# Attention on one core: VectorE's exponentials worked in 16-bit words, the order of the work kept

## The chip, the core and the metric

The kernel runs on one core of a Trainium2 chip. A core has five engines that each run their own queue in order: TensorE (PE in the profile, with its weight loads as PEld), VectorE (DVE), ScalarE (ACT), GpSimd (POOL) and SyncE (SP, which issues DMAs). The metric is the device time of one execution in microseconds.

## The reference

For 8 batches of 8 heads, with 512 positions of 64 numbers each, all in float32:

```python
scale = 1.0 / np.sqrt(q.shape[-1])
scores = np.einsum('bhqd,bhkd->bhqk', q, k) * scale
scores = scores - scores.max(axis=-1, keepdims=True)
attn = np.exp(scores)
attn = attn / attn.sum(axis=-1, keepdims=True)
return np.einsum('bhqk,bhkd->bhqd', attn, v).astype(np.float32)
```

## The kernel before

The 64 heads are taken as 32 pairs g = 0 to 31. A pair's q, k and v come in by one DMA each (256 KB), and GpSimd casts them to float16 (`cast`, steps `cq`, `ck`, `cv`). Pairs up to 21 have q and k transposed by TensorE into PSUM (`T`) and copied out by VectorE (`C`, tiles `tp` and `tqk`); from pair 22 a DMA transposes them (`u`).

A score group m is two blocks of 128 keys by 512 queries, 1024 elements per partition. TensorE writes it into one of three PSUM buffers `st` (`S`, as in `S12.0`: group 12, buffer 0). There are four groups to a pair. Nearly all groups get their exponential from ScalarE in one instruction (L295), which writes a float16 tile `pt`. No maximum is subtracted; the sum comes from a column of ones beside v.

Fourteen groups get their exponential on VectorE instead, by bit work in fixed point: the integer part of the scaled score is to become the exponent, and a polynomial in the fraction corrects the mantissa. The table `KIND` lists them with four kinds. For kinds C, F and S two matmuls first add a constant to the scores (the lift, L275), so that the bits of the 32-bit word in PSUM can be read as two halves. Each such group runs as steps between other work:

- `r` (`raise_`, L317): a pass over `st` that writes `z`, 32 bits;
- `p.0`, `p.1`, `p.2` (`pass_`, L350 and L331): passes that read halves of `st` or `z`, the intermediate `y`, and at last write the result, `pd` (32-bit words, of which TensorE reads every other half) or `pt`;
- for kinds S and X `m` (`middle`, L365 and L368) in the place of `p.1`: two instructions on GpSimd.

So ten groups (C and F) take four VectorE passes, and four groups (S and X) take three and two of GpSimd.

The values step `V` multiplies a block of 128 queries with v: four matmuls into one of seven places of an accumulator `o`, one of two PSUM banks that the transposes use as well. When seven are done, VectorE takes the reciprocal of the sums (`R`, tile `rc`) and multiplies (`N`, into `ring`); a DMA stores whole heads (`O`).

What runs after what on each engine is written out by hand as one list of steps, `ORDER`; every engine's queue follows it. A step such as `ck7+p12.2` is a cast that may not start before that VectorE step has ended.

```python
    def cast_behind(name, g, behind):
        ins = cast(g, name)
        if behind:
            tc.add_manual_dep(ins.ins, named[behind].ins.name, SYNC, reason="SBUF ports")
```

Of the kernel before, what the change touches and what calls it, by code (L numbers as in the profile page):

```python
# [8 lines left out]
FP32 = mybir.dt.float32  # L9
FP16 = mybir.dt.float16  # L10
U16 = mybir.dt.uint16
U32 = mybir.dt.uint32

LIFTED = "CFS"

EXP = mybir.ActivationFunctionType.Exp
AluOp = mybir.AluOpType
# [3 lines left out]
KIND = {5: "C", 12: "C", 20: "C", 30: "C", 39: "C", 47: "C", 57: "F", 68: "S", 72: "C", 81: "C", 93: "X", 99: "S", 108: "X", 111: "C"}  # L21
# [34 lines left out]
ck23 V11.0.3.95.0 T19.1.1 V11.1.0.96.0 cq24 V11.1.1.97.0 S71.1 R91.7 S72.0 m68.0 N91.7 S73.2 u22 C19  # L56
# [16 lines left out]
cv25+C2 V20.0.0.164.1 S98.2 N154.7 S99.1 m93.0 u29 S100.0 r99 V20.0.1.165.1 V20.0.2.166.1  # L73
# [3 lines left out]
V22.0.0.180.1 V22.0.1.181.1 S104.1 O133.1 R175.7 m99.0 S105.0 N175.7 V22.0.2.182.0 O147.1  # L77
# [7 lines left out]
N203.7 lv31 V24.1.3.215.0 m108.0 S117.0 p111.0 O189.1 V26.1.0.216.0 V26.1.1.217.1 O203.1  # L85
# [15 lines left out]
def kernel(  # L101
# [7 lines left out]
    nc = tc.nc  # L109
    B, H, S, D = q.shape  # L110
    P = 128
    NI = S // P
    assert NI == 4 and D == 64 and S == 512
    scale = float(D) ** -0.5
    LOG2E = 1.4426950408889634
# [14 lines left out]
    raises = {}  # L130
    for m, kind in KIND.items():
        (g, c, _), (g2, c2, _) = groups[m]
        assert 0 < g == g2 < LAST and c == c2
        if kind in LIFTED:
            raises.setdefault(g, set()).add(c)
# [6 lines left out]
    dpool = ctx.enter_context(tc.tile_pool(name="pd", bufs=4))  # L142
# [10 lines left out]
    lift = cpool.tile([P, P], FP16, name="lift")  # L153
# [10 lines left out]
    raised = {}  # L164
# [26 lines left out]
    def cast(g, name):  # L191
        if g >= NP:
            return
        if name == "v":
            return nc.gpsimd.tensor_copy(  # L195
                out=vps[g % NV][:, :, :, 0:D], in_=raw[g]["v"][:, :, :, :]
            )
        if g not in qkp:
            qkp[g] = qpool.tile([P, 2, NI, P], FP16, tag="qkp", name=f"qkp_{g}")
        dst = qkp[g][:, "qk".index(name)].rearrange("p i (h d) -> p h i d", h=2)  # L200
        src = raw[g][name]
        if (g, name) == (1, "q"):
            dve(nc.vector.tensor_copy(out=dst[:, :, 0:2], in_=src[:, :, 0:2]))
            return nc.gpsimd.tensor_copy(out=dst[:, :, 2:4], in_=src[:, :, 2:4])
        if name == "k" and g in raises:
            return nc.gpsimd.tensor_scalar(  # L206
                out=dst, in0=src[:, :, :, :], scalar1=128.0 * LOG2E, scalar2=1.0, op0=AluOp.mult, op1=AluOp.mult
            )
        return nc.gpsimd.tensor_copy(out=dst, in_=src[:, :, :, :])  # L209
# [7 lines left out]
    def dve(ins):  # L217
        latest[:] = [ins]
        return ins
# [42 lines left out]
    def scores(m, b):  # L262
        grp, kind = groups[m], KIND.get(m)
        half = m - len(groups) + 2
        cols = slice(256 * half, 256 * half + 256) if half >= 0 else slice(0, S)
        st = buffer(b, f"st_{m}")
        if kind in ("X", "Q"):
            bits = ppool.tile([P, 2, S], U16, tag="pt", name=f"pt_{m}")
            pt = bits.bitcast(FP16)
        elif kind:  # L270
            bits = dpool.tile([P, 2, S], U32, tag="pd", name=f"pd_{m}")
            pt = bits.bitcast(FP16).rearrange("p x (s n) -> p x s n", n=2)[:, :, :, 0]
            for x, (_, _, h) in enumerate(grp):
                s = slice(64 * h, 64 * h + 64)
                nc.tensor.matmul(st[:, x, :], lift[s], ones[s, 0:S], start=True, stop=False)  # L275
        elif half == 1:
            pt = last["pt"]
        else:
            pt = last["pt"] = ppool.tile([P, 2, S], FP16, tag="pt", name=f"pt_{m}")
        for x, (g, c, h) in enumerate(grp):  # L280
            if g == 0:
                s = slice(64 * (c % 2), 64 * (c % 2) + 64)
                kc = first["kt"][s, h, c // 2, :]
                qc = first["qt"][s, h].rearrange("p i c -> p (i c)")
            else:
                s = slice(64 * h, 64 * h + 64)
                kc = tqk[g][s, 1, c * P : (c + 1) * P]
                qc = tqk[g][s, 0, :]
            nc.tensor.matmul(st[:, x, cols], kc, qc[:, cols], start=kind is None or kind not in LIFTED, stop=True)  # L289
            blocks[(g, c, h)] = pt[:, x, :]  # L290
        if kind:
            raised[m] = {"st": st, "bits": bits}
            return
        by = scale / (128.0 * LOG2E) if grp[0][0] in raises else scale
        nc.scalar.activation(  # L295
            out=pt[:, :, cols], in_=st[:, :, cols], func=EXP, scale=by
        )
# [7 lines left out]
    LIFT = (143.0 * 1024 / 32, 0.0, -4.0 / 64)  # L305
    CUBIC = (-1.00024088 * 2.0**16, 3.90705425 * 2.0**16, 7.78636933e-2 * 1024 * 2.0**-48)
    QUARTIC = (7.77974906 * 2.0**16, -8.78105033 * 2.0**32, 4.4655924e-3 * 1024 * 2.0**-64)

    def fraction(t):
        return t.bitcast(U16).rearrange("p x (s n) -> p x s n", n=2)[:, :, :, 0]  # L310

    def raise_(m):
        r, kind = raised[m], KIND[m]
        r["z"] = wpool.tile([P, 2, S], FP32, tag="z", name=f"z_{m}")
        lifted = kind in LIFTED
        dve(
            nc.vector.tensor_scalar(  # L317
                out=r["z"][:, :, :],
                in0=r["st"][:, :, :],
                scalar1=2.0**17 if lifted else 1.0 if groups[m][0][0] in raises else 128.0 * LOG2E,  # L320
                scalar2=None if lifted else 143.0 * 1024,
                op0=AluOp.max if lifted else AluOp.mult,
                **({} if lifted else {"op1": AluOp.add}),
            )
        )

    def pass_(m, s):
        r, kind = raised[m], KIND[m]
        if kind in ("X", "Q") and s == 2:
            dve(  # L330
                nc.vector.scalar_tensor_tensor(  # L331
                    out=r["bits"][:, :, :],
                    in0=r["z"][:, :, :],
                    scalar=-(2.0**17) - QUARTIC[2] * (QUARTIC[1] / 2) ** 2,
                    in1=r["y"][:, :, :],
                    op0=AluOp.add,
                    op1=AluOp.add,
                )
            )
            return  # L340
        f, low = fraction(r["z"]), fraction(r["st"])
        if s == 0:
            r["y"] = wpool.tile([P, 2, S], FP32, tag="y", name=f"y_{m}")
        y = r["y"][:, :, :]
        last = s == 2
        quartic = kind in ("S", "X")
        zero = low if kind in LIFTED else f
        one = low if kind == "C" else f
        dve(
            nc.vector.scalar_tensor_tensor(  # L350
                out=r["bits"][:, :, :] if last else y,
                in0=(zero, one, y)[s],
                scalar=(QUARTIC if quartic else CUBIC)[s],
                in1=(f, y, r["z"][:, :, :])[s],
                op0=AluOp.mult if last else AluOp.add,
                op1=AluOp.add if last else AluOp.mult,
            )
        )

    def middle(m, _):  # L360
        r, kind = raised[m], KIND[m]
        t = wpool.tile([P, 2, S], FP32, tag="t", name=f"t_{m}", bufs=1)

        def product(x, add, scale, by=None):
            nc.gpsimd.tensor_scalar(  # L365
                out=t[:, :, :], in0=x, scalar1=add, scalar2=scale, op0=AluOp.add, op1=AluOp.mult
            )
            nc.gpsimd.tensor_tensor(  # L368
                out=r["y"][:, :, :], in0=t[:, :, :], in1=t[:, :, :] if by is None else by, op=AluOp.mult
            )  # L370

        if kind == "S":
            product(r["y"][:, :, :], QUARTIC[1], 1.0, r["y"][:, :, :])
            return
        centre = QUARTIC[1] / 2
        if kind == "Q":
            r["y"] = wpool.tile([P, 2, S], FP32, tag="y", name=f"y_{m}")
            product(fraction(r["z"]), QUARTIC[0] / 2, 1.0)
            centre -= (QUARTIC[0] / 2) ** 2
        product(r["y"][:, :, :], centre, QUARTIC[2] ** 0.5)  # L380
# [185 lines left out]
    with tc.manual_schedule():  # L566
# [4 lines left out]
        nc.vector.memset(lift, LIFT[0])  # L571
        for p in (32, 96):
            nc.vector.memset(lift[p : p + 32], LIFT[1])
            nc.vector.memset(lift[p : p + 1], LIFT[2])
        for n in range(NV):
# [10 lines left out]
            "m": middle,  # L586
# [48 lines left out]
```

## Time and profile before

| what | value |
|---|---|
| median of 3 runs | 116.33 us (116.09 to 116.99) |
| profiled execution | 116.05 us, span 114.3 us |
| granted TensorE clock | 1.000 |
| ScalarE busy | 107.0 us (94%) |
| VectorE busy | 103.5 us (91%) |
| TensorE matmuls busy | 103.8 us (91%) |
| GpSimd busy | 76.5 us (67%) |
| GpSimd casts of v, mean | 768 ns, 32 of them |
| GpSimd casts of q, mean | 612 ns, 30 of them |

The span runs from the first instruction to the last; the execution's own time has some 1.75 us around it. A line of the profile names the source line, the engine, the operation and `out<-in`. In a timeline the first number is the start, the second the duration, both in us, and in brackets stands the idle time before, with what ended it. Merged instructions show as xcount. Successive instructions of one engine overlap a little, so the distance from start to start is a better price than the duration.

### The profile page before, as it was taken

The page shows a single profiled execution, that of the slowest core. Times are in us where ns is not written, and L with a number is a line of the kernel's source. Part 1 is how long each engine was busy: PE and PEld are TensorE (multiplying, and loading weights), DVE is VectorE, ACT ScalarE, POOL GpSimd, SP SyncE. Part 2 cuts the span into 40 slices and gives each one's busy share as a digit, 9 for nine tenths or more (in the row PEclk, how much of TensorE's full clock was granted, in tenths as well). Part 3 has the DMA queues.
Part 4 walks back from the last instruction along what each step waited for, and adds up shares of the span by engine and source line. Part 5 has one row for each costly group of instructions (what it writes and reads, how often), then busy time and mean ns, then how long its engine had stood idle before and what let it go on. Part 6 is the DMA issues. An engine that isn't in the chain of part 4 may idle for free.

```text
span 114.3 us, 3938 instructions
## 1 busy us (share of the span) xinstructions
PE 103.8 (91%) x1549; PEld 65.7 (57%) x1549; DVE 103.5 (91%) x178; ACT 107.0 (94%) x119; POOL 76.5 (67%) x110
## 2 busy tenths in 40 slices
PE   7979899998899898999998899999999999999970
PEld 5635555565564564655665466675567666676660
DVE  4457999999999999999999999999999999999660
ACT  4499999999999999999999999999999999999960
POOL 2348755295968957927749999991799999384300
PEclk9999999999999999999999999999999999999999
DMA  2999999999999999999999998989959899999864
GB/s 92 276 317 373 384 380 382 383 385 373 384 388 367 363 382 382 372 384 388 373 376 383 373 215 260 172 267 384 272 147 312 238 327 151 383 333 366 290 231 146
DMA packets 45619, 36.44 MB, mean 319 GB/s; under 512 B 12704, under 2 KB 45600, under 8 KB 45600
## 3 DMA queue, kind: packets, MB, share of 16 engines
q1 hardware_dynamic: 45168, 35.86, 103.8%
q10 hardware_dynamic: 432, 0.33, 0.9%
q8 instruction: 12, 0.20, 0.6%
q14 instruction: 7, 0.06, 0.1%
HBM read 25.17 MB, written 8.39 MB: 294 GB/s over the span
## 4 chain that ended last, share of the span: by engine, by line
DVE 32%; PE 31%; ACT 26%; issue 5%; DMA 2%; ACTq 0%
ACT pt L295 24%; PE o L420 14%; PE st L289 13%; DVE y L350 12%; DVE tqk L254 5%; DVE ring L393 4%; DVE pd L350 4%; DVE z L317 4%; DMA q<-in_q_dram 2%; ACT pt L527 2%; DVE rc L385 1%; PE tp L234 1%; PE o L430 1%; DVE obl L461 1%; PE st L275 0%
## 5 line engine op out<-in xcount | busy, mean ns | idle before, releaser
L295 ACT ACTIVATE pt<-st 128x1024 f16<-128x1024 f32 (+1 forms) x112 | 102.1, 1113 | 0.4 <-PE st L289 0.4
L289 PE MATMUL st<-tqk 64*128 64x512 f16 (+1 forms) x250 | 47.0, 380 | 5.2 <-ACT pt L295 3.3
L420 PE MATMUL o<-vp,pt 128*128 128x65 f16 x912 | 45.4, 195 | 0.0
L420 PEld LDWEIGHTS <-pt 128*128 128x128 f16 x912 | 36.2, 98 | 14.4 <-issue 13.3
L195 POOL CAST vp<-v 128x512 f16<-128x512 f32 x32 | 24.1, 768 | 10.4 <-DVE pd L350 4.2
L289 PEld LDWEIGHTS <-tqk 64*128 64x128 f16 x250 | 14.4, 93 | 17.9 <-issue 8.2
L393 DVE TENSOR_TENSOR ring<-o,rc 128x448 f32<-128x448 f32 (+2 forms) x37 | 22.5, 608 | 1.0 <-DVE rc L385 0.2
L209 POOL CAST qkp<-q 128x512 f16<-128x512 f32 x30 | 18.1, 612 | 2.9 <-DVE rc L385 1.4
L317 DVE TENSOR_SCALAR z<-st 128x1024 f32<-128x1024 f32 x14 | 17.0, 1213 | 1.3 <-PE st L289 1.1
L209 POOL CAST qkp<-k 128x512 f16<-128x512 f32 x19 | 13.6, 719 | 5.7 <-issue 2.4
L350 DVE SCALAR_TENSOR_TENSOR pd<-y,z 128x1024 uint32<-128x1024 f32 x12 | 15.3, 1272 | 0.0
L420 PE MATMUL o<-vp,pd 128*128 128x65 f16 x96 | 15.1, 195 | 0.1
L350 DVE SCALAR_TENSOR_TENSOR y<-st,z 128x1024 f32<-128x1024 uint16 x12 | 14.5, 1212 | 0.0
L234 PE MATMUL tp<-ident,qkp 128*128 128x128 f16 x168 | 14.0, 220 | 0.4 <-POOL qkp L206 0.4
L254 DVE COPY tqk<-tp 128x1024 f16<-128x1024 f16 x20 | 13.6, 681 | 0.1
L234 PEld LDWEIGHTS <-qkp 128*128 128x128 f16 x168 | 9.7, 97 | 4.0 <-issue 1.7
L420 PEld LDWEIGHTS <-pd 128*128 128x128 f16 x96 | 9.4, 98 | 2.8 <-issue 2.2
L350 DVE SCALAR_TENSOR_TENSOR y<-st,y 128x1024 f32<-128x1024 uint16 x9 | 10.9, 1208 | 0.0
L206 POOL TENSOR_SCALAR qkp<-k 128x512 f16<-128x512 f32 x12 | 7.4, 617 | 5.0 <-DVE pd L350 3.5
L385 DVE RECIPROCAL rc<-o 128x7 f32<-128x7 f32 (+2 forms) x37 | 7.2, 196 | 1.5 <-PE o L420 1.3
L365 POOL TENSOR_SCALAR t<-y 128x1024 f32<-128x1024 f32 x4 | 4.2, 1044 | 2.4 <-DVE y L350 2.1
L368 POOL TENSOR_TENSOR y<-t,y 128x1024 f32<-128x1024 f32 x2 | 5.6, 2780 | 0.2
(57 smaller groups left out, 46.7 us busy)
## 6 DMA issues: line engine op xcount, KB each, us to landing
v<-in_v_dram SPq DMA_DIRECT2D x32, 256.0 KB, 5.4
k<-in_k_dram SPq DMA_DIRECT2D x31, 256.0 KB, 5.5
q<-in_q_dram SPq DMA_DIRECT2D x31, 256.0 KB, 5.4
out_dram<-ring SPq DMA_DIRECT2D x29, 256.0 KB, 4.5
out_dram<-ring SPq DMA_DIRECT2D x5, 128.0 KB, 3.5
k<-in_k_dram ACTq DMA_DIRECT2D x2, 128.0 KB, 2.7
q<-in_q_dram SPq DMA_DIRECT2D x2, 128.0 KB, 2.9
tqk<-qkp SPq DMA_TRANSPOSE x10, 5.3
```

What stands on the lines that cost most here:

```text
L195: return nc.gpsimd.tensor_copy(out=vps[g % NV][:, :, :, 0:D], in_=raw[g]["v"][:, :, :, :])
L206: return nc.gpsimd.tensor_scalar(out=dst, in0=src[:, :, :, :], scalar1=128.0 * LOG2E, scalar2=1.0, op0=AluOp.mult, op1=AluOp.mult)
L209: return nc.gpsimd.tensor_copy(out=dst, in_=src[:, :, :, :])
L234: nc.tensor.transpose(tps[g][:, n, i, :], qkp[g][:, n, i, :], ident)
L254: nc.vector.tensor_copy(out=tqk[g][:, :, :], in_=tps.pop(g).rearrange("p n i c -> p n (i c)"))
L289: nc.tensor.matmul(st[:, x, cols], kc, qc[:, cols], start=kind is None or kind not in LIFTED, stop=True)
L295: nc.scalar.activation(out=pt[:, :, cols], in_=st[:, :, cols], func=EXP, scale=by)
L317: nc.vector.tensor_scalar(out=r["z"][:, :, :], in0=r["st"][:, :, :], scalar1=2.0**17 if lifted else 1.0 if groups[m][0][0] in raises else ...
L350: nc.vector.scalar_tensor_tensor(out=r["bits"][:, :, :] if last else y, in0=(zero, one, y)[s], scalar=(QUARTIC if quartic else CUBIC)[s], ...
L385: dve(nc.vector.reciprocal(out=rcs[u][:, 0:n], in_=o[:, x : x + n, D : D + 1]))
L393: nc.vector.tensor_tensor(out=ring[:, u % NU : u % NU + n, :], in0=o[:, x : x + n, 0:D], in1=rc[:, 0:n].broadcast_to([P, n, D]), op=AluOp. ...
L420: nc.tensor.matmul(os[u // 7][:, u % 7, :], blocks[(g, c, h)][:, y * P : (y + 1) * P], vps[g % NV][:, h, c, :], start=(c == 0), stop=(c == ...
```

## The change

All fourteen groups take the same form, `ON_VECTOR` lists them without kinds. There is no lift, no scaled cast of keys, and GpSimd has no part in them. VectorE reads the scores from PSUM once and writes a 16-bit fixed-point word `x` (10 bits of fraction). Everything else is between 16-bit tiles in SBUF: `f` is the fraction by a mask, `h` and `g` are two factors (each an addition and a multiplication by constants on `f`), `y` is first `f*h`, then `y*g`, and the sum `x + y` is the bits of the float16 result `pk`. Step `r` now issues x and f, `p.0` h and a product, `p.1` g and a product, `p.2` the sum. In `ORDER` the four `m` steps become `p.1` at the same places; nothing else of it changes.

```diff
-KIND = {5: "C", 12: "C", 20: "C", 30: "C", 39: "C", 47: "C", 57: "F", 68: "S", 72: "C", 81: "C", 93: "X", 99: "S", 108: "X", 111: "C"}
+ON_VECTOR = (5, 12, 20, 30, 39, 47, 57, 68, 72, 81, 93, 99, 108, 111)
...
-    dpool = ctx.enter_context(tc.tile_pool(name="pd", bufs=4))
+    dpool = ctx.enter_context(tc.tile_pool(name="pk", bufs=6))
...
-    lift = cpool.tile([P, P], FP16, name="lift")
...
-        if name == "k" and g in raises:
-            return nc.gpsimd.tensor_scalar(
-                out=dst, in0=src[:, :, :, :], scalar1=128.0 * LOG2E, scalar2=1.0, op0=AluOp.mult, op1=AluOp.mult
-            )
...
-            for x, (_, _, h) in enumerate(grp):
-                s = slice(64 * h, 64 * h + 64)
-                nc.tensor.matmul(st[:, x, :], lift[s], ones[s, 0:S], start=True, stop=False)
...
     def raise_(m):
+        r = raised[m]
+        x = work(m, "x", U16)
         dve(
             nc.vector.tensor_scalar(
+                out=x,
                 in0=r["st"][:, :, :],
+                scalar1=scale * LOG2E * OCTAVE,
+                scalar2=15 * OCTAVE,
+                op0=AluOp.mult,
+                op1=AluOp.add,
+            )
+        )
+        dve(
+            nc.vector.tensor_scalar(
+                out=work(m, "f", U16), in0=x, scalar1=int(OCTAVE) - 1, scalar2=None, op0=AluOp.bitwise_and
             )
         )
 
     def pass_(m, s):
+        r = raised[m]
+        x, f = r["x"][:, :, :], r["f"][:, :, :]
+        if s == 2:
             dve(
+                nc.vector.tensor_tensor(
+                    out=r["bits"][:, :, :], in0=x, in1=r["y"][:, :, :], op=AluOp.add
                 )
             )
             return
+        w = work(m, "hg"[s], FP16)
+        dve(
+            nc.vector.tensor_scalar(
+                out=w,
+                in0=f,
+                scalar1=(-OCTAVE, CUBIC[1] * OCTAVE)[s],
+                scalar2=(1.0, CUBIC[0])[s] / OCTAVE,
+                op0=AluOp.add,
+                op1=AluOp.mult,
+            )
+        )
         if s == 0:
+            work(m, "y", FP16)
         y = r["y"][:, :, :]
+        dve(nc.vector.tensor_tensor(out=y, in0=(f, y)[s], in1=w, op=AluOp.mult))
...
-    def middle(m, _):
...
```

How the queues move shows best in VectorE's around group 20, at about 22 to 29 us of the trace before. Of before, from the copy ahead of the group's first pass to its last pass:

```order
L254 COPY tqk_511<-tp_0_512 128x1024
L317 TENSOR_SCALAR z_556<-st_504 128x1024
L385 RECIPROCAL rc_583<-o_530 128x7
L393 TENSOR_TENSOR ring<-o_530,rc_583 128x448
L350 SCALAR_TENSOR_TENSOR y_604<-st_504,z_556 128x1024
L254 COPY tqk_608<-tp_0_609 128x1024
L350 SCALAR_TENSOR_TENSOR y_604<-st_504,y_604 128x1024
L385 RECIPROCAL rc_675<-o_578 128x7
L393 TENSOR_TENSOR ring<-o_578,rc_675 128x448
L350 SCALAR_TENSOR_TENSOR pd_505<-y_604,z_556 128x1024
```

The same stretch of the changed kernel:

```order
L301 TENSOR_SCALAR x_556<-st_506 128x1024
L311 TENSOR_SCALAR f_558<-x_556 128x1024
L345 RECIPROCAL rc_585<-o_530 128x7
L353 TENSOR_TENSOR ring<-o_530,rc_585 128x448
L328 TENSOR_SCALAR h_606<-f_558 128x1024
L340 TENSOR_TENSOR y_608<-f_558,h_606 128x1024
L243 COPY tqk_612<-tp_0_613 128x1024
L328 TENSOR_SCALAR g_657<-f_558 128x1024
L340 TENSOR_TENSOR y_608<-y_608,g_657 128x1024
L345 RECIPROCAL rc_681<-o_580 128x7
L353 TENSOR_TENSOR ring<-o_580,rc_681 128x448
L321 TENSOR_TENSOR pk_507<-x_556,y_608 128x1024
```

Four passes have become seven at the same places; only the first reads PSUM, and three read what stands directly ahead of them.

GpSimd's queue in the last third of the program, of before (v pairs 25, 24 and 26, then q and k of pair 31, with the middle steps of groups 93 and 99):

```order
L195 CAST vp_87<-v_25_1843 128x8x64
L365 TENSOR_SCALAR t_2078<-y_2033 128x1024
L368 TENSOR_TENSOR y_2033<-t_2078 128x1024
L195 CAST vp_86<-v_24_1793 128x8x64
L195 CAST vp_88<-v_26_1803 128x8x64
L365 TENSOR_SCALAR t_2199<-y_2145 128x1024
L368 TENSOR_TENSOR y_2145<-t_2199,y_2145 128x1024
L209 CAST qkp_2318<-q_31_1723 128x2x4x64
```

And of the changed kernel:

```order
L188 CAST vp_87<-v_25_1875 128x8x64
L188 CAST vp_86<-v_24_1823 128x8x64
L188 CAST vp_88<-v_26_1835 128x8x64
L198 CAST qkp_2358<-q_31_1751 128x2x4x64
L198 CAST qkp_2358<-k_31_1782 128x2x4x64
```

The casts stand in the same order, without the two middle steps between them.

103 lines of the change are left out of this document (22 added, 81 removed).

## The prediction

> **What bounds the kernel now.** I read the page's busy shares first, then the two engines near 100% as timelines, then the chain that ended last.
>
> ```profile
> PE 103.8 (91%) x1549; PEld 65.7 (57%) x1549; DVE 103.5 (91%) x178; ACT 107.0 (94%) x119; POOL 76.5 (67%) x110
> ```
>
> ```profile
> 5.42 0.60 ACT L527 ACTIVATE pt<-st_0a 128x512 f16<-128x512 f32 x1 [0.99 <-PE st_0a L520]
> ...
> 8.22 101.52 ACT L295 ACTIVATE pt<-st 128x1024 f16<-128x1024 f32 x111
> 110.11 0.60 ACT L295 ACTIVATE pt<-st 128x512 f16<-128x512 f32 x1 [0.37 <-PE st L289]
> ```
>
> ScalarE runs from 5.42 us to 110.7 us with one gap of 0.37 us. The change leaves ScalarE the same 119 instructions, so nothing that becomes quicker elsewhere can take more from the middle than this gap; a gain has no room. A loss has: VectorE (DVE) is just as full, which the table of stretches shows (stretch and its length, then busy us of PE, PE's weight loads, DVE, ScalarE and GpSimd).
>
> ```profile
> 20.00:30.00 10.00, 9.40 (x138) 5.63 (x135) 9.92 (x16) 10.00 (x12) 6.59 (x10) 1.00 1.09 381
> ...
> 60.00:70.00 10.00, 8.93 (x130) 5.63 (x128) 9.93 (x13) 10.00 (x12) 9.51 (x12) 1.00 1.11 316
> ...
> 100.00:110.00 10.00, 9.99 (x194) 6.89 (x190) 8.28 (x16) 9.74 (x12) 4.72 (x5) 1.00 1.02 330
> ```
>
> DVE is busy 9.9 of 10 us up to the last stretch. In the chain of waits DVE pieces follow each other from 11.15 to 34.64 us and from 38.71 to 49.6 us; from 50 us ScalarE and then PE carry it.
>
> ```profile
> 11.15 0.18 DVE rc L385
> ...
> 34.64 0.74 PE st L289 x4
> ...
> 48.93 0.69 DVE tqk L254
> ...
> 85.02 0.21 PE st L275 x2
> ...
> 94.20 0.22 PE st L275 x2
> ```
>
> So in the first half every microsecond that DVE loses shows in the end, unless ScalarE's next scores already stand in PSUM. The question is what DVE's queue costs after the change.
>
> **Prices of DVE's operations.** One group in program order, group 20, next to what GpSimd (POOL) does at that time:
>
> ```profile
> 21.87 0.68 DVE L254 COPY tqk<-tp 128x1024 f16<-128x1024 f16 x1
> 22.47 1.21 DVE L317 TENSOR_SCALAR z<-st 128x1024 f32<-128x1024 f32 x1
> 23.61 0.19 DVE L385 RECIPROCAL rc<-o 128x7 f32<-128x7 f32 x1
> 23.83 0.62 DVE L393 TENSOR_TENSOR ring<-o,rc 128x448 f32<-128x448 f32 x1
> 24.37 1.21 DVE L350 SCALAR_TENSOR_TENSOR y<-st,z 128x1024 f32<-128x1024 uint16 x1
> 25.50 0.68 DVE L254 COPY tqk<-tp 128x1024 f16<-128x1024 f16 x1
> 26.10 1.21 DVE L350 SCALAR_TENSOR_TENSOR y<-st,y 128x1024 f32<-128x1024 uint16 x1
> 27.23 0.19 DVE L385 RECIPROCAL rc<-o 128x7 f32<-128x7 f32 x1
> 27.46 0.63 DVE L393 TENSOR_TENSOR ring<-o,rc 128x448 f32<-128x448 f32 x1
> 28.00 1.22 DVE L350 SCALAR_TENSOR_TENSOR pd<-y,z 128x1024 uint32<-128x1024 f32 x1
> ...
> 29.84 0.19 DVE L385 RECIPROCAL rc<-o 128x7 f32<-128x7 f32 x1
> 29.95 1.17 DVE L317 TENSOR_SCALAR z<-st 128x1024 f32<-128x1024 f32 x1
> ```
>
> ```profile
> 22.20 0.62 POOL L206 TENSOR_SCALAR qkp<-k 128x512 f16<-128x512 f32 x1 [3.47 <-DVE pd L350]
> 22.88 0.61 POOL L209 CAST qkp<-q 128x512 f16<-128x512 f32 x1
> 23.43 0.62 POOL L195 CAST vp<-v 128x512 f16<-128x512 f32 x1
> ...
> 28.04 1.65 POOL L209 CAST qkp<-k 128x512 f16<-128x512 f32 x1
> ```
>
> From start to start, a pass over 1024 elements in 32 bits takes 1.13 us (24.37 to 25.50) and a 16-bit copy of 1024 takes 0.60 (21.87 to 22.47). An instruction that reads what the one just before it wrote starts 0.11 us later than one that doesn't: 23.61 to 23.83 is 0.22, 29.84 to 29.95 is 0.11. An undisturbed cast takes 0.61 and the next one starts 0.55 after it.
>
> The page has no 16-bit operation from SBUF to SBUF. Two rows bound it.
>
> ```profile
> L493 DVE CAST q<-q 128x256 f16<-128x256 f32 x1 | 0.3, 297 | 1.2 <-DMA q<-in_q_dram 1.2
> ...
> L560 DVE COPY qt<-tp_qb 128x512 f16<-128x512 f16 x1 | 0.4, 425 | 0.0
> ```
>
> ```profile
> L393 DVE TENSOR_TENSOR ring<-o,rc 128x256 f32<-128x256 f32 x1 | 0.4, 424 | 0.0
> ```
>
> One source in SBUF (L493: 256 elements in 297 ns) beats the 32-bit pass from PSUM (256 in 424) by about half, and 16 bits halve it too. If both count, 1024 elements cost as much as 512 of L560: 425 ns, or 0.34 from start to start (its successor starts 0.08 before its end, as above). The upper bound is 0.60, the 16-bit copy. For two 16-bit sources the nearest row is that copy, 0.60; the upper bound is 1.13. I take 0.34 and 0.60: all operands of these six have 16 bits, like the rows.
>
> **The change part by part.** Per group it now issues seven instructions: x from PSUM (1.13, 32-bit input as before), f, h, g with one source (3 x 0.34), two products and the sum (3 x 0.60). Three of them read what the instruction directly before wrote (f, and each product): 3 x 0.11. That makes 1.13 + 1.02 + 1.80 + 0.33 = 4.28 us.
> - Ten groups (kinds C and F) spent 4 x 1.13 = 4.52 on DVE: 10 x -0.24 = -2.4 us.
> - Four groups (S and X) spent 3 x 1.13 = 3.39, since GpSimd did the middle: 4 x +0.89 = +3.6 us.
> - Waits at the port that DVE has now and that are counted anew below: the last pass at 77.03 us took 1.61 and that at 94.32 took 1.51 instead of 1.21, and one at 83.14 took 1.39: -0.9 us.
>
> Without collisions DVE's queue is therefore +0.3 us: the 16-bit form saves nothing worth naming, because 0.33 us go to waits of DVE on itself and four groups lose GpSimd's help.
>
> Then the collisions. The rows that show them:
>
> ```profile
> 76.95 0.61 POOL L209 CAST qkp<-k 128x512 f16<-128x512 f32 x1
> ```
>
> ```profile
> 77.03 1.61 DVE L350 SCALAR_TENSOR_TENSOR pd<-y,z 128x1024 uint32<-128x1024 f32 x1
> ...
> 83.14 1.39 DVE L350 SCALAR_TENSOR_TENSOR y<-z 128x1024 f32<-128x1024 uint16 x1
> ...
> 94.32 1.51 DVE L350 SCALAR_TENSOR_TENSOR pd<-y,z 128x1024 uint32<-128x1024 f32 x1
> ```
>
> ```profile
> 6.57 0.29 DVE L203 CAST qkp<-q 128x256 f16<-128x256 f32 x1
> 6.60 0.52 POOL L204 CAST qkp<-q 128x256 f16<-128x256 f32 x1 [0.41 <-DMA q<-in_q_dram]
> ```
>
> A cast that began 0.04 us after a DVE pass with two SBUF sources (28.00) ended 0.47 us after it: it stood until DVE was done. A pass that began 0.08 us after a cast (76.95) was longer by 0.40. So whichever comes second waits out the other. A pass that reads one operand from PSUM overlaps casts freely: 24.37 took 1.21 with casts all through it. Today one pass of a C group is exposed (p2); after the change six of seven are: the products and the sum surely, the one-source three if a DVE copy within SBUF blocks too. L204's cast, 0.52 us under a DVE cast where 256 elements lie between 0.29 (128) and 0.61 (512), about 0.40, says that it does.
>
> ```profile
> L496 POOL CAST k<-k 128x128 f16<-128x128 f32 x1 | 0.3, 291 | 2.1 <-DMA k<-in_k_dram 2.1
> ```
>
> The Trainium skill ("SBUF — State Buffer", Who interferes with whom) has this as a rule: a DVE operation in a two-port mode, or with two SBUF inputs, and a GpSimd operation exclude each other for whole instructions. The rows above agree for two inputs; for one-source 16-bit operations no row here shows it.
>
> I walk group 20 with these prices; the key cast is a plain cast now, so casts start at 22.20, 22.75, 23.31 and 23.87. x runs 22.47 to 23.60. f is ready at 23.71 and waits for a cast until 23.87 (0.16). Reciprocal and normalisation from PSUM run to 24.97 while the next casts run to 25.32: h waits 0.35. Its product is ready at 25.77, but GpSimd took the port at 25.66 when h let go: 0.45. C7's copy, then g and its product meet no cast, since GpSimd's next one is tied to a later reciprocal. The sum is ready at 29.23 and finds a cast that began at 29.15: 0.48. Together 1.4 us, so group 20 ends 1.2 us later than now. The floor is 0, the ceiling six whole casts, 3.3 us. GpSimd is busy 6.6 and 9.5 of 10 us in the two earlier stretches above; part of the second were the middle steps, which go, so casts cover somewhat over half the time. I take 1.1 us for each of the eleven groups up to 95 us and 0.3 for the last three, where few casts are left: 13 us.
>
> What hides some of it: DVE's own gaps at the end,
>
> ```profile
> 106.62 0.20 DVE L385 RECIPROCAL rc<-o 128x7 f32<-128x7 f32 x1 [0.52 <-PE o L420]
> ...
> 109.28 0.21 DVE L385 RECIPROCAL rc<-o 128x7 f32<-128x7 f32 x1 [0.81 <-PE o L420]
> ```
>
> 0.52 + 0.81 = 1.3 us, and in the second half some 2 us of tolerance: 256 row blocks in about 104 us make 2.8 us for the seven blocks of the other accumulator bank, less 0.8 for reciprocal and normalisation. Beyond it PE stands at a bank that isn't free, its score matmuls stand behind, and ScalarE starves: two scores ahead of it are 1.8 us of work, at 101.52 / 111 = 0.91 each.
>
> The other edits are free. The lift matmuls (0.21 us for a pair in the chain) and the scaling of key casts go from engines that wait for ScalarE or DVE for most of the time; the score bank is released after x, but the order gives it to nobody earlier. Five start memsets go where DVE then waits 1.2 us for the first input anyway (L493's row).
>
> **The sum.** The profiled execution took 116.05 us, its span of 114.3 and 1.75 around it: 116.05 + 0.3 + 13 - 1.3 - 2.0 = 126.05. It lies 0.28 below the median of the runs, 116.33, so I say 126.3 us. The rivals are reckoned from that median.
>
> **The rivals.**
> - *One-source operations don't take the port.* Then only three of seven collide: waits halve to 6.5 us, 116.33 + 0.3 + 6.5 - 3.3 = 119.8. For it: no row has such a 16-bit operation. Against it: L204. Without the skill's rule the sum would be this one. Chance 0.17.
> - *Absorbed: ScalarE keeps the end.* If waits stay under 0.3 us per group, 4 us in all, the 3.3 us of cover leave at most 1 us of them: 116.6. For it: many casts are tied to a DVE step, and GpSimd loses the middle steps. Against it: the walk. Chance 0.13.
> - *Faster: PE is relieved.* From 84 us the chain runs on PE, where two lift pairs (0.21 and 0.22) go, and ScalarE's last gap of 0.37 may close: 0.8 in all: 115.5 with no wait at DVE, and a little more if PE's scores come earlier. This decides only if DVE is not late at 84 us. Chance 0.03.
> - *The 16-bit forms run slower.* One source at 0.60: 3 x 0.26 = 0.78 more in each of 14 groups, 126 + 11 = 137; two sources at 1.13 too: 4.28 becomes 6.65, 2.37 x 14 = 33 us more than 126, less part of the waits: about 150. Against it: L493 and the 16-bit copies. Chance 0.11 together.
>
> **Numbers.** The forecast keeps 0.56. Its own bounds are waits of 0.6 to 2.0 us per group, 120 to 136. The range goes down to 116.5, over the first rival and half of the second, and up to 136; the slow forms stay out. A measurement here tells about 1% from no change: faster 0.03 (the PE case), same 0.13 (absorbed), slower 0.84 (the rest).
>
> **What would show it.** Right: f, h, g rows with 0.4 us at their shortest and means well above it; products of 0.68 at their shortest; GpSimd casts of more than 0.61 all over; ScalarE with gaps after PE's scores, the first within 11 to 50 us; DVE in the chain to the end. Wrong: f, h or g never under 0.68, casts still at 0.61, or ScalarE's 111 instructions again in one piece.

## The result, and the profile after

The changed kernel takes 128.38 us (median of 4 runs, 127.59 to 129.34) against 116.66 us of the kernel before timed beside it (4 runs, 116.09 to 117.03): a ratio of 1.101, interval 1.092 to 1.111. The prediction said 126.3 us. The profiled execution took 127.59 us, its span 125.8 us; that is 11.5 us more than before in both.

The page's busy shares and the granted clock in 40 slices of the changed kernel:

```profile
PE 103.7 (82%) x1525; PEld 65.4 (52%) x1525; DVE 112.3 (89%) x219; ACT 109.7 (87%) x119; POOL 66.9 (53%) x102
...
PEclk9999999999999999999999558999999999999997
```

The same 119 instructions of ScalarE now fill 87% instead of 94%. VectorE (DVE) is busy for 8.8 us more, its waits at the port included. The clock row shows a dip that the kernel before doesn't have; it is taken up below.

ScalarE's timeline, which was one piece of 101.52 us before (start, duration, in brackets the idle time before and what ended it):

```profile
7.82 5.71 ACT L279 ACTIVATE pt<-st 128x1024 f16<-128x1024 f32 x6
13.74 1.94 ACT L279 ACTIVATE pt<-st 128x1024 f16<-128x1024 f32 x2 [0.21 <-PE st L274]
...
52.76 17.19 ACT L279 ACTIVATE pt<-st 128x1024 f16<-128x1024 f32 x18 [0.56 <-PE st L274]
73.07 2.12 ACT L279 ACTIVATE pt<-st 128x1024 f16<-128x1024 f32 x2 [3.12 <-PE st L274]
```

ScalarE breaks into 14 pieces, each ended by TensorE's scores; the first gap comes at 13.7 us. Who holds TensorE, the chain of waits tells by engine, before and after:

```profile
DVE 32%; PE 31%; ACT 26%; issue 5%; DMA 2%; ACTq 0%
```

```profile
DVE 68%; PE 20%; issue 5%; DMA 3%; SPq 1%; POOL 0%
```

VectorE carries most of it, with breaks: TensorE has it from 70.97 to 78.69 us, from 84.81 to 90.37 and from 113.06 to 120.78.

VectorE's operations of the fourteen groups, grouped by shape (busy us, mean ns of one, idle us before them):

```profile
L301 DVE TENSOR_SCALAR x<-st 128x1024 uint16<-128x1024 f32 x14 | 16.9, 1209 | 1.4 <-PE st L274 1.4
...
L340 DVE TENSOR_TENSOR y<-f,h 128x1024 f16<-128x1024 uint16 x14 | 12.0, 854 | 0.5
L340 DVE TENSOR_TENSOR y<-y,g 128x1024 f16<-128x1024 f16 x14 | 11.4, 814 | 0.5
L321 DVE TENSOR_TENSOR pk<-x,y 128x1024 uint16<-128x1024 uint16 x14 | 10.2, 728 | 0.0
L328 DVE TENSOR_SCALAR h<-f 128x1024 f16<-128x1024 uint16 x14 | 9.3, 663 | 0.0
L311 DVE TENSOR_SCALAR f<-x 128x1024 uint16<-128x1024 uint16 x14 | 7.3, 522 | 0.5
L328 DVE TENSOR_SCALAR g<-f 128x1024 f16<-128x1024 uint16 x14 | 6.9, 495 | 0.0
```

x takes what the first pass took before (1213 ns). The other six lie above their shortest, which the end of the timeline shows, when GpSimd has only five casts left to do after 100 us:

```profile
110.03 0.42 DVE L328 TENSOR_SCALAR g<-f 128x1024 f16<-128x1024 uint16 x1
110.48 0.69 DVE L340 TENSOR_TENSOR y<-y,g 128x1024 f16<-128x1024 f16 x1
111.09 0.42 DVE L328 TENSOR_SCALAR h<-f 128x1024 f16<-128x1024 uint16 x1
```

So an undisturbed factor takes 0.42 us and an undisturbed product 0.69. Against 420 and 684 ns (alone, experiment 5) the six means are too long by 102, 243, 75, 170, 130 and 44 ns (f, h, g, the two products, the sum): 764 ns a group, 10.7 us in fourteen. The other party shows it too, GpSimd's casts, of which an undisturbed one took 0.61 us before:

```profile
L198 POOL CAST qkp<-k 128x512 f16<-128x512 f32 x31 | 23.7, 774 | 11.1 <-PE st L274 3.6 <-issue 3.2 <-DMA k<-in_k_dram 2.3
L188 POOL CAST vp<-v 128x512 f16<-128x512 f32 x32 | 23.1, 739 | 31.9 <-DVE pk L321 17.3 <-DVE rc L345 5.5 <-DVE f L311 5.1
L198 POOL CAST qkp<-q 128x512 f16<-128x512 f32 x30 | 20.9, 706 | 4.5 <-DVE rc L345 2.9 <-DVE y L340 1.1 <-DMA q<-in_q_dram 0.6
```

The collisions in group 20, VectorE first and then GpSimd:

```profile
24.33 0.47 DVE L311 TENSOR_SCALAR f<-x 128x1024 uint16<-128x1024 uint16 x1
...
25.49 0.62 DVE L328 TENSOR_SCALAR h<-f 128x1024 f16<-128x1024 uint16 x1
26.14 0.98 DVE L340 TENSOR_TENSOR y<-f,h 128x1024 f16<-128x1024 uint16 x1
```

```profile
23.91 0.62 POOL L188 CAST vp<-v 128x512 f16<-128x512 f32 x1
24.47 0.81 POOL L198 CAST qkp<-k 128x512 f16<-128x512 f32 x1
25.22 0.61 POOL L198 CAST qkp<-q 128x512 f16<-128x512 f32 x1
25.78 0.80 POOL L188 CAST vp<-v 128x512 f16<-128x512 f32 x1
26.53 1.07 POOL L198 CAST qkp<-k 128x512 f16<-128x512 f32 x1
```

The cast at 23.91 runs beside x (23.09 to 24.30) and isn't disturbed. h at 25.49 meets the cast of 25.22 and is 0.20 us too long; the cast of 25.78 meets h and is 0.19 too long; the product at 26.14 meets that cast (+0.30); the cast of 26.53 meets the product (+0.46). Each engine holds up the other in turn.

### The profile page after: what moved, and what is told of

It is laid out like the page before. It is cut to its first block, busy times and chain, and to the rows that moved or that the text cites. A ratio compares the mean times of both kernels' runs of the same rounds, so it can differ in the third digit from the quotient of the medians.

```text
span 125.8 us, 3915 instructions
## 1 busy us (share of the span) xinstructions
PE 103.7 (82%) x1525; PEld 65.4 (52%) x1525; DVE 112.3 (89%) x219; ACT 109.7 (87%) x119; POOL 66.9 (53%) x102
## 4 chain that ended last, share of the span: by engine, by line
DVE 68%; PE 20%; issue 5%; DMA 3%; SPq 1%; POOL 0%
DVE y L340 14%; DVE ring L353 12%; DVE x L301 11%; PE o L380 9%; DVE tqk L243 9%; PE st L274 8%; DVE h L328 6%; DVE f L311 5%; DVE pk L321 4%; DVE g L328 4%; DMA k<-in_k_dram 3%; DVE rc L345 3%; PE tp L223 2%; SPq L435 1%; PE o L390 1%
## 5 line engine op out<-in xcount | busy, mean ns | idle before, releaser
L198 POOL CAST qkp<-k 128x512 f16<-128x512 f32 x31 | 23.7, 774 | 11.1 <-PE st L274 3.6
L274 PEld LDWEIGHTS <-tqk 64*128 64x128 f16 x250 | 12.2, 93 | 18.2 <-issue 5.8
L301 DVE TENSOR_SCALAR x<-st 128x1024 uint16<-128x1024 f32 x14 | 16.9, 1209 | 1.4 <-PE st L274 1.4
L380 PE MATMUL o<-vp,pk 128*128 128x65 f16 x112 | 16.5, 196 | 0.8 <-DVE ring L353 0.7
L380 PEld LDWEIGHTS <-pk 128*128 128x128 f16 x112 | 10.5, 98 | 4.0 <-issue 2.0
L340 DVE TENSOR_TENSOR y<-f,h 128x1024 f16<-128x1024 uint16 x14 | 12.0, 854 | 0.5
L340 DVE TENSOR_TENSOR y<-y,g 128x1024 f16<-128x1024 f16 x14 | 11.4, 814 | 0.5
L321 DVE TENSOR_TENSOR pk<-x,y 128x1024 uint16<-128x1024 uint16 x14 | 10.2, 728 | 0.0
L328 DVE TENSOR_SCALAR h<-f 128x1024 f16<-128x1024 uint16 x14 | 9.3, 663 | 0.0
L311 DVE TENSOR_SCALAR f<-x 128x1024 uint16<-128x1024 uint16 x14 | 7.3, 522 | 0.5
L328 DVE TENSOR_SCALAR g<-f 128x1024 f16<-128x1024 uint16 x14 | 6.9, 495 | 0.0
```

The costliest lines, as they stand in the source:

```text
L274: nc.tensor.matmul(st[:, x, cols], kc, qc[:, cols], start=True, stop=True)
L301: nc.vector.tensor_scalar(out=x, in0=r["st"][:, :, :], scalar1=scale * LOG2E * OCTAVE, scalar2=15 * OCTAVE, op0=AluOp.mult, op1=AluOp.add,)
L321: nc.vector.tensor_tensor(out=r["bits"][:, :, :], in0=x, in1=r["y"][:, :, :], op=AluOp.add)
L328: nc.vector.tensor_scalar(out=w, in0=f, scalar1=(-OCTAVE, CUBIC[1] * OCTAVE)[s], scalar2=(1.0, CUBIC[0])[s] / OCTAVE, op0=AluOp.add, op1=A ...
L340: dve(nc.vector.tensor_tensor(out=y, in0=(f, y)[s], in1=w, op=AluOp.mult))
L380: nc.tensor.matmul(os[u // 7][:, u % 7, :], blocks[(g, c, h)][:, y * P : (y + 1) * P], vps[g % NV][:, h, c, :], start=(c == 0), stop=(c == ...
```

## The experiments

The theory on test: the time is lost in VectorE's queue, most of it as waits for GpSimd's casts. The rivals: one-source operations don't collide; the waits of VectorE on itself or the lost middle steps of GpSimd are the main part; a few late places on TensorE, and the dip of its clock, make the loss. All ratios are to runs of the kernel before beside the experiment's own (medians 116.19 us for experiments 1 to 4, 116.67 for 5 and 6, 116.49 for 7 to 9, 116.61 for 10).

**1. Only x.** All work on 16-bit tiles is left out; x itself is the result.

```diff
-        x = work(m, "x", U16)
+        x = r["bits"][:, :, :]
...
     def pass_(m, s):
+        return
```

> The changed kernel with only x left of a VectorE group: x is written straight into the result's tile, and f, h, g, both products and the sum are left out (VectorE loses about 50 us, the fourteen exponentials are only a straight line per octave). Everything else stays. Theory (ScalarE is the floor that the kernel before already stood on, VectorE's queue is what the change made late): 115.5 to 116.3 us, ScalarE again in one piece. Rival (TensorE was the limit and lift and buffers matter): under 115 us. Rival (something else of the change costs, such as the cast order or the buffers): stays above 118 us.

A cast that was tied to a pass that is left out waits for that group's x instead; the same holds for experiments 8 and 9, and in experiment 7 it waits for the pass before.

Measured: 116.34 us, ratio 1.000 (0.997 to 1.004). The profiled execution is the longest of the ten, 118.45 us.

```profile
PE 102.2 (88%) x1525; PEld 65.0 (56%) x1525; DVE 63.1 (54%) x135; ACT 107.4 (92%) x119; POOL 55.7 (48%) x102
```

```profile
8.51 86.53 ACT L279 ACTIVATE pt<-st 128x1024 f16<-128x1024 f32 x94
```

VectorE has 40 us less to do than before, and the median time is the same. ScalarE runs in one piece up to 95 us; this long execution then has gaps of 1.04, 0.61 and 0.36 us. So ScalarE is the floor, even this much less work on VectorE doesn't go below it, and the whole 10% come with f, h, g, the products and the sum.

**2. Small casts.** The changed kernel with GpSimd's casts cut from 512 to 64 columns after the first pairs, so that the casts seldom hold the port. The 16-bit tiles of q and k are six fixed ones, so that the other columns keep older values.

```diff
+        if name == "v" and g >= NV:
+            return nc.gpsimd.tensor_copy(
+                out=vps[g % NV][:, 0:1, 0:1, 0:D], in_=raw[g]["v"][:, 0:1, 0:1, :]
+            )
...
+        if g > QK16:
+            dst, src = dst[:, 0:1, 0:1], src[:, 0:1, 0:1]
+            return nc.gpsimd.tensor_copy(out=dst, in_=src)
```

> The changed kernel with every GpSimd cast of q and k from pair 7 on and of v from pair 12 on cut to 64 of its 512 columns (the other columns keep what an earlier pair left there). VectorE's instructions and all DMAs stay the same; GpSimd holds the port an eighth as many columns per cast. Theory (collisions at the port): VectorE's waits, 11.1 us over the shortest instructions of its own profile, nearly vanish: 117.5 us, 116.3 to 119.5. Rival (it is the seven instructions and their waits on each other): 126 to 128 us. Rival (GpSimd's casts were not late, TensorE's clock dip is what costs): 124 us or more with the dip still there.

Measured: 121.2 us, ratio 1.045 (1.042 to 1.048).

```profile
L348 DVE TENSOR_TENSOR y<-f,h 128x1024 f16<-128x1024 uint16 x14 | 10.3, 733 | 0.5
...
L336 DVE TENSOR_SCALAR h<-f 128x1024 f16<-128x1024 uint16 x14 | 6.2, 441 | 0.0
```

With f 439, g 421, the second product 713 and the sum 694, the same reckoning as above gives that 1.8 us of waits are left and 8.9 are gone. The time falls by 1.101 - 1.045 = 5.6 points, 6.5 us. GpSimd's work falls too, from 66.9 to 34.8 us, but in the changed kernel's chain GpSimd has 0%, so most of the 6.5 us is put down to the port. The expected 117.5 us was missed: 5.2 us over before remain, more than the waits that are left, although VectorE is now busy for only 103.9 us against 103.5 before. Part of this is where VectorE's work stands in its queue. ScalarE's gaps of 0.94 us at 92.47 us and of 0.88 at 107.25 are in the changed kernel as well (0.94 at 98.41, 0.88 at 114.23), and ahead of each TensorE stood for a normalisation (0.85 and 0.84 us here, 0.96 and 0.84 there). Before, ScalarE has no such gap.

**3. The same cut in the kernel before**, as a control, with the scaling of key casts dropped in the small ones and the rest.

```diff
-        if name == "k" and g in raises:
+        if g > QK16:
+            dst, src = dst[:, 0:1, 0:1], src[:, 0:1, 0:1]
+            return nc.gpsimd.tensor_copy(out=dst, in_=src)
+        if name == "k" and g in ():
```

> The control: the kernel before with its casts cut in the same way (and keys not scaled for the lift). Theory: it has 0.9 us of waits at the port and ScalarE is its floor: 115.8 to 116.5 us, no change. If small casts by themselves make a kernel quicker by several us, the run on the changed kernel tells less: then below 115 us here.

Measured: 118.44 us, ratio 1.018 (1.012 to 1.023). Missed: smaller casts alone make the kernel before some 2 us slower. The profiled execution is the longest of the four, 119.88 us. In it one of the two last passes of the X kind, 1237 ns before, takes 3.17 us (from 92.29 us) beside one of GpSimd's middle steps:

```profile
L339 DVE SCALAR_TENSOR_TENSOR pt<-z,y 128x1024 uint16<-128x1024 f32 x2 | 4.4, 2196 | 0.0
```

These are 1.9 us in the two, and ScalarE has a gap of 1.22 us behind them, at 97.91 us. It also has gaps of 0.56, 0.26 and 0.49 us before 12.75 us, where the granted clock is 0.50 from 10 to 12 us. The changed kernel has no middle steps, so the 2 us can't simply be taken off experiment 2. What is sure: cutting the casts isn't neutral. So 6.5 us is what the cut took off the changed kernel, not the exact size of what the collisions cost, and whether it is too low or too high is not shown.

**4. Both factors directly behind each other.** g is computed right after h, so that the factor and its product no longer depend on the instruction directly before.

```diff
+            for n in range(2):
+                dve(
+                    nc.vector.tensor_scalar(
+                        out=work(m, "hg"[n], FP16),
...
+        w = r["hg"[s]][:, :, :]
```

> The changed kernel with g computed directly behind h, in the first step instead of the second: h, g, product, and later only the product. Same instructions; no product stands directly behind its factor, so two of three waits of VectorE on itself go (14 x 0.22 = 3.1 us). Self-waits alone: 125.3 us. If a cast also uses that gap to take the port between a factor and its product (the theory's 0.45 us a time, 4 us in all in the profile): 123 us, 121.5 to 124.5. If neither matters because casts just collide elsewhere: 127.5 us or more.

Measured: 127.61 us, ratio 1.097 (1.091 to 1.102), not told apart from the changed kernel.

```profile
L341 DVE TENSOR_TENSOR y<-y,g 128x1024 f16<-128x1024 f16 x14 | 10.5, 748 | 0.0
...
L329 DVE TENSOR_SCALAR g<-f 128x1024 f16<-128x1024 uint16 x14 | 8.7, 625 | 0.0
```

The idle time ahead of the products, 0.5 us in all for each of the two rows, is gone, but g now waits for casts (495 to 625 ns): with f 550, h 618, the first product 856 and the sum 735 the waits add up to 11.5 us instead of 10.7. What VectorE doesn't wait for itself, it waits at the port.

**5. The prices alone.** No attention is computed: each operation eight times in a row on tiles of this size, first alone, then while GpSimd runs eight casts of 128x512, then while it fills 128x512 with a constant, which only writes.

```diff
+                for n in range(8):
+                    if phase == "cast":
+                        ins = nc.gpsimd.tensor_copy(out=g16[n % 4][:, :], in_=flat)
+                    else:
+                        ins = nc.gpsimd.memset(g16[n % 4][:, :], 1.0)
...
+                for n in range(8):
+                    ins = form(what, o[n % 4][:, :])
```

> A kernel for durations only: it computes no attention (it copies one tile of q to the output) and runs each of six VectorE forms of 1024 elements eight times: x (from PSUM), f, h, product, sum, and a 32-bit pass with two SBUF sources; first alone, then beside eight GpSimd casts of 512 columns, then beside eight GpSimd fills of the same tile that read nothing. Theory: alone x 1.13 from start to start, f and h 0.34, product and sum 0.60, 32-bit pass 1.13. Beside casts all but x alternate with them, about 0.55 more per pair of instructions; x does not. Rival (one-source forms do not take the port): f and h beside casts as alone. By the skill's rule (SBUF - State Buffer, Who interferes with whom) fills hold up f and h but not products, sums and the 32-bit pass.

Measured (136.25 us in all, of no interest), the second of four outputs of each form; the middle word of the name is the phase, d is the 32-bit form with two sources:

```profile
L72 DVE TENSOR_SCALAR f_alone_b<-x 128x1024 uint16<-128x1024 uint16 x2 | 0.8, 420 | 0.0
L72 DVE TENSOR_SCALAR f_cast_b<-x 128x1024 uint16<-128x1024 uint16 x2 | 1.7, 832 | 0.0
L72 DVE TENSOR_SCALAR f_fill_b<-x 128x1024 uint16<-128x1024 uint16 x2 | 1.6, 820 | 0.0
L80 DVE TENSOR_TENSOR y_alone_b<-f,h 128x1024 f16<-128x1024 uint16 x2 | 1.4, 683 | 0.0
L80 DVE TENSOR_TENSOR y_cast_b<-f,h 128x1024 f16<-128x1024 uint16 x2 | 2.2, 1094 | 0.0
L80 DVE TENSOR_TENSOR y_fill_b<-f,h 128x1024 f16<-128x1024 uint16 x2 | 1.4, 684 | 0.0
L83 DVE SCALAR_TENSOR_TENSOR d_alone_b<-z,w 128x1024 f32<-128x1024 f32 x2 | 2.4, 1217 | 0.0
L83 DVE SCALAR_TENSOR_TENSOR d_cast_b<-z,w 128x1024 f32<-128x1024 f32 x2 | 3.3, 1627 | 0.0
L68 DVE TENSOR_SCALAR x_cast_b<-st 128x1024 uint16<-128x1024 f32 x2 | 2.4, 1216 | 0.0
```

The one-source 16-bit operation collides with casts like the others, which ends the rival at 119.8 us; x from PSUM does not. In this steady alternation a collision makes each form longer by the same 0.41 us. Fills collide with f but not with two-source operations. The Trainium skill ("SBUF — State Buffer", Who interferes with whom) has this distinction: a two-source operation meets GpSimd's reads, a one-source operation in a two-port mode meets both. The trace agrees. The page also says that the second fully blocks for the whole instruction; the start-to-start times differ from that:

```profile
52.57 0.83 DVE L72 TENSOR_SCALAR f_cast_c<-x 128x1024 uint16<-128x1024 uint16 x1
53.32 0.83 DVE L72 TENSOR_SCALAR f_cast_d<-x 128x1024 uint16<-128x1024 uint16 x1
...
65.44 1.09 DVE L80 TENSOR_TENSOR y_cast_c<-f,h 128x1024 f16<-128x1024 uint16 x1
66.45 1.09 DVE L80 TENSOR_TENSOR y_cast_d<-f,h 128x1024 f16<-128x1024 uint16 x1
```

An f and a cast together take 0.75 us and not 0.34 + 0.56 = 0.90, a product and a cast 1.01 and not 0.60 + 0.56 = 1.16. About 0.15 us of each pair overlaps.

**6. The four S and X groups back in 32 bits**, with GpSimd's middle steps (four result buffers instead of six, 27 score tiles instead of 30).

```diff
+    OLD = (68, 93, 99, 108)
...
     def raise_(m):
+        if m in OLD:
+            return raise_old(m)
```

> The changed kernel with groups 68, 93, 99 and 108 back in the 32-bit form whose middle steps run on GpSimd (three VectorE passes, no lift; four result buffers in place of six and 27 score tiles in place of 30, for room). The ten other groups stay in the 16-bit form. By my sum the four groups cost 4 x 0.89 = 3.6 us of VectorE's queue and some waits: 124.5 us. If the loss comes only from collisions in the first half: 127 to 128 us. If the four groups carried most of it: 121 us or less.

Measured: 127.43 us, ratio 1.091 (1.086 to 1.095), hardly less than the changed kernel.

```profile
L386 DVE TENSOR_TENSOR y<-f,h 128x1024 f16<-128x1024 uint16 x10 | 10.5, 1048 | 0.3
...
L374 DVE TENSOR_SCALAR h<-f 128x1024 f16<-128x1024 uint16 x10 | 7.8, 779 | 0.0
```

With f 694, g 497, the second product 806 and the sum 682, ten groups now wait 12.0 us: more than fourteen did. GpSimd has 80.8 us of work instead of 66.9, and its middle steps seem to hold the port as well (the last pass of these groups takes 1411 ns, against 1217 alone in experiment 5). For the price of the four groups alone the run says nothing.

**7. Half the polynomial.** g and the second product are left out (a square takes the place of the cubic).

```diff
-        w = work(m, "hg"[s], FP16)
+        if s == 1:
+            return
+        w = work(m, "h", FP16)
```

> The changed kernel with a polynomial of one degree less: g and the second product are left out, y = f * 0.34 (f - 1) in octaves, so a group is x, f, h, one product and the sum (five instructions, four of them at the port). Theory (VectorE's queue plus its collisions set the time): 14 x (0.45 + 0.60) = 14.8 us of queue go and some 3 us of waits, more than the 12 us of loss: ScalarE's floor again, 116.0 to 117.5 us. Rival (TensorE's stalls and clock dip, or the casts' lateness, are the cause and not the queue's length): 121 us or more.

Measured: 119.15 us, ratio 1.024 (1.020 to 1.028): 7.7 points or 9 us less than the changed kernel, but 1.6 us above the upper end expected. The waits per operation stay (f 572, h 601, product 814, sum 695: 6.6 us in all), while ScalarE waits only 1.9 us for scores, in five gaps. So this much shorter queue no longer holds ScalarE up much in the middle, and what remains over before isn't explained by those gaps alone.

**8 and 9. The full form in the first seven groups only (5 to 57), or in the last seven only (68 to 111)**, the others with x alone.

```diff
+    def plain(m):
+        return m > 57
...
-        x = work(m, "x", U16)
+        x = r["bits"][:, :, :] if plain(m) else work(m, "x", U16)
```

> The full 16-bit form only in groups 5 to 57; in groups 68 to 111 only x is left, written into the result (f, h, g, products and sum left out there). Theory: in the profile of the changed kernel ScalarE stands four exponentials behind at 53 us, 4 us: 120.3 us, 119.5 to 121.5. If the first half hides its loss (two scores ahead in PSUM): under 118 us. If nearly all comes from here: over 125 us.

> The reverse: only x in groups 5 to 57, the full 16-bit form in groups 68 to 111. Theory: the rest of the loss, 8 us, if the two halves simply add: 124 us. If the second half's loss is mostly the lateness that it inherits: under 120 us, and then the halves do not add up to the 12 us.

Measured: 120.86 us, ratio 1.038 (1.034 to 1.043), and 123.87 us, ratio 1.065 (1.059 to 1.072). Against 116.49 us these are 4.4 and 7.4 us; together 11.8, the loss of the whole change. In the first of the two, ScalarE has its gaps up to 53 us, and then:

```profile
52.65 52.09 ACT L279 ACTIVATE pt<-st 128x1024 f16<-128x1024 f32 x56 [0.56 <-PE st L274]
```

VectorE is busy 13.7 of 20 us from 60 to 80 us there and 12.2 of 20 from 80 to 100, yet nothing is won back, since ScalarE is full. A loss in either half goes to the end whole.

**10. One late copy moved ahead.** At 70 us of the changed kernel TensorE stands for a copy, and its clock falls. The rows of TensorE, and stretches of 2 us (busy us of PE, its weight loads, DVE, ScalarE, GpSimd, then the clock):

```profile
67.25 0.39 PE L274 MATMUL st<-tqk 64*128 64x512 f16 x2 [0.19 <-ACT pt L279]
68.16 0.39 PE L274 MATMUL st<-tqk 64*128 64x512 f16 x2 [0.52 <-ACT pt L279]
70.97 0.58 PE L223 MATMUL tp<-ident,qkp 128*128 128x128 f16 x4 [2.41 <-DVE tqk L243]
```

```profile
68.00:70.00 2.00, 0.39 (x2) 0.19 (x2) 1.97 (x5) 1.95 (x3) 2.00 (x3) 0.88 1.32 178
70.00:72.00 2.00, 1.03 (x13) 1.03 (x13) 2.00 (x3) 0.00 (x0) 0.82 (x2) 0.50 1.58 100
...
74.00:76.00 2.00, 2.00 (x26) 1.34 (x24) 1.93 (x4) 1.42 (x3) 2.00 (x3) 0.50 1.14 328
```

The copy is moved from behind the second product of group 68 to ahead of it:

```diff
-... S72.0 p68.1 N91.7 S73.2 u22 C19
+... S72.0 C19 p68.1 N91.7 S73.2 u22
```

> The changed kernel with one step of the order moved: VectorE's copy C19 stands ahead of group 68's second factor and product instead of behind them and the normalisation, so that TensorE's transposes for pair 20, which wait for it (2.41 us, at 70.97 us of the changed kernel's trace), start some 2 us earlier; VectorE's work is the same. If the dip of the granted clock (0.50 from 70 to 76 us) and ScalarE's 3.12 us of idle time there cost time of their own, the wait at 70 us falls to about 0.5 us, the clock stays at 0.99 or more there, and the time falls by 2 to 3 us, to a ratio of 1.075 to 1.085. If VectorE's queue alone sets the end and the dip only falls into time that is lost anyway, the dip goes but the ratio stays within 1 percent of the changed kernel's 1.10.

Measured: 128.3 us, ratio 1.099 (1.095 to 1.104). The wait for the copy is gone, but the next step in TensorE's queue then stands for the normalisation, which the product still holds up:

```profile
68.97 0.38 PE L223 MATMUL tp<-ident,qkp 128*128 128x128 f16 x4 [0.19 <-DVE tqk L243]
71.15 0.26 PE L380 MATMUL o<-vp,pt 128*128 128x65 f16 x3 [1.80 <-DVE ring L353]
```

The dip is shorter (0.55 and 0.60 in the stretches from 72 to 76 us, 1.00 otherwise), so the expectation that it would go was wrong, and ScalarE's longest gap falls from 3.12 to 2.05 us. The time stays. The rows above point to the reason: VectorE is busy 1.93 to 2.00 of every 2 us through the dip, and from 10 to 85 us it is busy 73.5 of 75 us with the longer dip as with the shorter. It hardly waits for anyone there, neither for TensorE nor for a late cast. So the gap is where ScalarE finds out how late VectorE is, and no loss of its own is seen. The changed kernel's four runs fit this: the two with the higher mean clock (0.987 and 0.986) took 128.62 and 129.34 us, the two with 0.966 took 127.59 and 128.14. Experiment 4's longest run, 129.44 us, has its lowest clock, 0.956, so the runs alone don't settle it. A kernel with the same queue and no dip at all was not had.

## Why the prediction was right, point by point

- **No room for a gain; VectorE's queue decides.** Shown by experiments 1, 8 and 9. The step "in the first half every microsecond that DVE loses shows in the end" held, and by these two runs it held for the second half as well.
- **Prices.** Right: 0.42 us a factor (0.34 from start to start) and 0.68 a product (0.60) when alone. One reading behind them was loose: L493's 297 ns are 30% less than 424, not half, so the rows alone didn't give 0.34. From the undisturbed rows a group costs 4.31 us (x with its step to f 1.25, f 0.34, h and g 0.45 each with the product's wait on them, products 0.61 each, sum 0.60); the prediction said 4.28.
- **Queue without collisions, +0.3 us.** With 4.31 it is -2.1 + 3.7 - 0.9 = +0.7. The +0.89 for each S and X group, which experiment 6 could not show, fits experiments 8 and 9: the seven groups of the first half (C and F) save 7 x 0.21 = 1.5 us and wait 6.0 by their rows (f 579, h 743, g 495, products 896 and 774, sum 686), which makes 4.5 against 4.4 measured; the last seven wait 4.7, pay 4 x 0.92 = 3.7, save 3 x 0.21 = 0.6 and the 0.9 of old waits: 6.9 against 7.4. The 0.7 can be set beside the page: VectorE's 8.8 us more of busy time, 1.5 of idle time ahead of f and the products and 0.7 for the five start memsets that went make 11.0, where queue and waits (0.7 and 10.7) make 11.4.
- **Collisions, 13 us: too much.** The rows give 10.7. The walk of group 20 had 1.4 us where the trace shows 0.05 (f), 0.20 (h) and 0.30 (first product). These three came where the walk had them, each 0.11 to 0.15 shorter: it charged the whole rest of a cast each time, and experiment 5 shows some 0.15 us of overlap in a colliding pair. Its last wait, 0.48 at the sum, didn't come at all: the sum began at 29.47 us, 0.05 ahead of the cast, and the cast waited (1.11 us). A full collision costs 0.41, not 0.55.
- **Cover, 3.3 us: none of it is seen.** This is the step that the runs bear out least. By steps as measured, 116.05 + 0.7 + 10.7 = 127.45, and the profiled execution took 127.59. The 1.3 us of VectorE's end gaps were not used: after the change these gaps are 0.39, 0.78 and 0.89 us, from 115.83 us on. They don't take late work from 80 us earlier, because ScalarE can't run faster afterwards. Of the 2 us of tolerance counted for the other accumulator bank and the scores that stand ahead nothing is seen either: ScalarE has 13 gaps, and they begin at 13.7 us. But the sum isn't exact enough to say that this tolerance was nil. The same reckoning from 116.05 gives 118.55 us for experiment 2 (0.7 + 1.8), 125.15 for experiment 4 (0.7 - 3.1 + 11.5) and 125.95 for experiment 6 (-2.1 + 12.0). Their profiled executions took 121.26, 127.24 and 128.37 us: 2.1 to 2.7 us more. Local stands such as those of experiment 2 are not in it, and in the changed kernel they may balance a cover.
- **The number.** By these figures the errors (2.3 too much wait, 3.3 too much cover, 0.4 too little queue) nearly cancel, so the 126.3 is nearer than its terms, and that part is luck. The range from 116.5 to 136 us held more than one mechanism (the first rival's 119.8 lies in it), so the rows and the experiments bear the mechanism out, not the range. A small slip in the working: the "absorbed" rival allows up to 1 us beyond its cover, so its time is 116.3 to 117.3, where 116.6 stands.
- **The rivals.** One source without the port: refuted by experiment 5 and by the means of f, h and g. Absorbed, and faster by a relieved TensorE: refuted by the time. Slow 16-bit forms: refuted, 0.34 and 0.60 from start to start.
- **What would show it.** f, h and g at some 0.4 at their shortest and 0.5 to 0.66 in the mean, products from 0.68, casts of 0.71 to 0.77, ScalarE's first gap at 13.7 us: all as said. VectorE has 68% of the chain, but not "to the end": TensorE carries three stretches, the last one from 113.06 us. Not foreseen were the dip and the stand of TensorE before it.

What stays open: the remaining 5.2 us of experiment 2, of which its own waits are 1.8 and the queue 0.7 to 1.6 (with or without the old waits), while the rest, 1.8 to 2.7, is only in part traced to stands behind single normalisations; how far the tolerance of the second half covered anything; and the dip's own price, against which speak VectorE's full queue and the four runs. No version beat both kernels.

## What to carry to other kernels

Before one wide operation is split into several cheap ones, ask which of them touch memory that another engine's port shares: six short operations within SBUF can each collide where of a C group's four passes only the one without a PSUM operand could, and the sum of durations alone (4.31 against 4.52 us) says nothing about it. Where an engine downstream is full from start to end, don't count gaps that come after the delay as cover for a queue that feeds it: here a delay in either half arrived whole. A collision is priced from both engines' rows, since each delays the other and the pattern of the casts moves with it.

## What the runs showed of the hardware that was not expected

- TensorE's granted clock fell to 0.50 for six us after a time in which it had hardly worked: 0.39 of 2 us from 68 to 70, a stand of 2.41 us. It fell again in experiment 10 after a stand of 1.80 us (to 0.55), and in experiments 4, 6 and 9 after stands of 1.99, 1.96 and 1.99 us. It did not fall so in experiments 2, 7 and 8, whose longest stands are 1.17 us or less and whose clocks are 0.999, 0.995 and 0.993 in the mean. The length of the stand alone doesn't decide: one of 1.89 us in experiment 6, at 76 us, left the clock at 1.00. The Trainium skill ("TensorE: Matmul & The Clock Gate", Part 1: The HAM clock gate) says that an idle window of about 3.4 us halves the clock. Here the stand itself was shorter; the stretch with one pair of scores alone, from 67.64 to 70.97 us by the rows of experiment 10's section, was 3.3 us, but the clock was already below 1 (0.88) in the stretch from 68 to 70.
- A cast and a VectorE operation that collide take 0.15 us less together than one after the other (0.75, 1.01), and a GpSimd fill holds up one-source but not two-source operations.
